# Output projection of a hybrid decoder layer: its last two column parts as one part of 1024 columns, with seven products for four pairs of k-tiles

## The chip, the cores and the metric

The kernel runs on one core of a Trainium2 chip. The time is device microseconds (us) from the start to the end of one execution. Before the change it is 1035.69 us, the median of 3 runs (1035.39 to 1035.95).

## The reference, cut to what matters

One decoder layer on a sequence of 256 tokens with model width 2048, everything in float32. Two attention blocks (A: dilated sliding windows, B: latent attention, each 8 heads of 128 columns) give `mixed`, 256 tokens by 2048 columns, of which block A is the first 1024. Then comes the part that the change touches, and the feed-forward part after it:

```python
mixed = jnp.concatenate([a_out.reshape(B, S, DSWA_HEADS * HEAD_DIM),
                         b_out.reshape(B, S, MLA_HEADS * V_HEAD_DIM)], axis=-1)
x = x + _rmsnorm(mixed @ w_out[layer], norm_attn_post[layer])      # w_out: 2048 x 2048

h = _rmsnorm(x, norm_mlp_pre[layer])
u = jnp.square(jax.nn.relu(h @ w_up[layer]))                       # w_up: 2048 x 8192
x = x + _rmsnorm(u @ w_down[layer], norm_mlp_post[layer])          # w_down: 8192 x 2048
```

## The kernel before, in words

**Precision by three products.** TensorE multiplies a rounded format here. Every float32 operand is therefore split into two tiles, `hi` (the rounded value, written by ScalarE) and `lo` (what is left, written by VectorE: `lo = raw - hi`), and every product is three matmuls: hi·hi, lo·hi, hi·lo (`split` L308, and `split_gain` L314 where a gain is multiplied in). A matmul takes 128 rows of k, 128 tokens and 512 columns. The two blocks of 128 tokens are called b = 0 and b = 1, a k-tile is 128 rows of a weight.

**The stream of weights.** `Weights` (L180 on) holds all weight tiles of the kernel as one planned list. A tile is 128 x 1024 numbers; its loading is one DMA of 512 KB on SP's queue into one of 5 `raw` buffers, and its split fills one of 8 `hi` and one of 8 `lo` buffers. `get(i)` (L227), called just ahead of the matmuls that use tile i, writes into the program all loads and splits up to tile i + 6 (`W_AHEAD`), never more than 8 tiles beyond the first one that is not yet done with. So the place of a split in VectorE's and ScalarE's program is six tiles ahead of its use; each engine works through its own program in the order written.

**The order of everything else.** A `Flow` counts the time of the matmuls written so far. Chains of other work (the softmax of a head, the evacuation of a result) are generators; a `yield 1.5` means that the next step is written into the program when the count has gone on by 1.5 us. `flow.pump()` behind each group of three matmuls writes what is due.

**The output projection** (L915 to L939). `mixT` (hi and lo) holds `mixed` transposed, 16 k-tiles. `w_out` is cut in four column parts n = 0 to 3 of 512 columns, each of 8 tiles of two k-tiles. The parts 0 and 1 run together, first the k-tiles 0 to 11, then 12 to 15, since the last heads of block B are still being computed meanwhile. Then part 2 runs, then part 3. In part 3 the last five tiles are done for b = 0 first, then for b = 1, so that the work on b = 0 can begin 30 matmuls before the end. Every part accumulates in one PSUM bank for each b.

At the first finished result the pool `pb` of block B is given back, and the gain `g_post` (1 MB, one row sent to 128 partitions) is loaded by SP's queue into the room that was freed (L930). `powers` (L848) starts there too: four squares of `g_post` on ScalarE, small operations, and four multiplications of 128 x 1024 of the residual `x` on VectorE (L869). `out_evac` (L831) takes a finished bank: a square with its sum on ScalarE (L835), a multiplication by `g_post` on VectorE (L836). When a b has all four parts, `residual(b)` (L872) computes the norm, updates `x`, and transposes it for the up projection, whose first five k-tiles run for b = 0 ahead of b = 1.

**Seven products.** The up and the down projection already use Strassen's scheme (in Winograd's form) for some pairs of k-tiles. A pair of k-tiles, two blocks of tokens and two halves of 512 columns are a 2 x 2 block product; instead of 8 block products it takes 7, of three matmuls each. For that, `seven` (L351) makes two tiles `t` and `u` of sums of the raw weights on VectorE and gives the stream four tiles: `b11` (half a tile), `b`, `u` and `t`. The operands on the left need four sums of blocks, split too. Three of the four results are had only from four extra accumulators m1, m6, m7, m5, which `close` (L1110) turns into three tiles that are added to the banks once. `seven_products` (L1094) writes the 21 matmuls.

Of the kernel before, what the change touches and what calls it, by code (L numbers as in the profile page):

```python
# [18 lines left out]
F32 = mybir.dt.float32  # L19
# [94 lines left out]
UP_STEPS = [up_steps(range(16))] + [THREE] * 7  # L114

# [153 lines left out]
def layer(nc, tc, io):  # L269
    flow = Flow()  # L270

    def pool(name, side, **kw):
        return tc.alloc_tile_pool(name=name, bufs=1, side=side, **kw)
# [70 lines left out]
    for n, m in ((0, 6), (1, 6), (0, 2), (1, 2), (2, 8), (3, 8)):  # L344
        ch_o[n].plan(m)
# [75 lines left out]
    wide_u, after = [], 0  # L421
# [307 lines left out]
    kv_chain = flow.start(latent(ckv, 0, "kv", lat), 2.0)  # L729
# [4 lines left out]
    pb = pool("pb", "right")  # L734

# [15 lines left out]
    latT["q"] = [pb.tile([P, 4, S], F32R, name=f"cqT_{w}") for w in ("hi", "lo")]  # L751
# [70 lines left out]


# [89 lines left out]

    res = [None] * NB
    for ns in ((0, 1), (2,), (3,)):  # L915
        if len(ns) == 2:
            order = [(c, t, b) for ts in (range(6), range(6, 8)) for c in range(2) for t in ts for b in range(NB)]
        else:
            order = [(0, t, b) for t, b in in_order(8, (0, APART[0] if ns == (3,) else 0))]
        for c, b, acc in proj(mixT, [ch_o[n] for n in ns], f"o{ns[0]}", order, heads_done):  # L920
            n = ns[c]
            if not late:
                flow.finish(*pair_chain)
                pb.release()
# [3 lines left out]
                po = late["po"] = pool("po", "right")  # L928
                late["g_post"] = po.tile([P, D], F32, name="g_post")
                nc.sync.dma_start(out=late["g_post"],  # L930
                                  in_=io["norm_attn_post"].partition_broadcast(P).rearrange("p o d -> p (o d)"))
                late["yg"] = [po.tile([P, D], F32, name=f"yg{b}") for b in range(NB)]
                pw_chain = flow.start(powers())
            out_evac(n, b, acc[0])
            if n == 3:
                flow.finish(pw_chain)
                weights.ahead = AHEAD_NORM
                res[b] = flow.start(residual(b), b * D_SECOND)
                flow.pump()  # L939
# [149 lines left out]
    def three(out, a, w, first, last):  # L1089

        for i, (x, y) in enumerate(((0, 0), (0, 1), (1, 0))):
            mm(out, a[x], w[y], first and i == 0, last and i == 2)

    def seven_products(ts, left, accs, m, first, last, m_first=False):  # L1094

        (a11, a12, a22), (s3, s1, s2, s4) = left
        prods = ((a11, 0, 0, 1), (a12, 1, 0, (0, 0)), (s4, 1, 1, (0, 1)), (s2, 2, 0, 6), (a22, 2, 1, (1, 0)),
                 (s3, 3, 1, 7), (s1, 3, 0, 5))
        if m_first:
            prods = sorted(prods, key=lambda x: not isinstance(x[3], int))  # L1100
        for p, (a, i, half, to) in enumerate(prods):
            w = weights.get(ts[i])
            in_m = isinstance(to, int)
            three(m[to] if in_m else accs[to], a, [w[x][:, half * 512:half * 512 + 512] for x in range(2)],
                  in_m and first, in_m and last)
            if all(x[1] != i for x in prods[p + 1:]):
                weights.free(ts[i])
            flow.pump()

    def close(c, m):  # L1110

# [279 lines left out]
```

## Time and profile before

| | before |
|---|---|
| median of the runs | 1035.69 us |
| profiled execution: its own time | 1035.85 us |
| profiled execution: span of the instructions | 1034.1 us |
| TensorE busy | 1022.4 us, 99% |
| VectorE busy | 834.4 us, 81% |
| ScalarE busy | 634.6 us, 61% |
| GpSimd busy | 63.5 us, 6% |
| first and last matmul of the output projection start at | 254.3 and 354.8 us |
| matmuls of the output projection | 384 |

The span runs from the first to the last instruction; 1.75 us of the execution's own time lie around it. "PE" is TensorE, "DVE" VectorE, "ACT" ScalarE, "POOL" GpSimd, "SP" the engine that issues most transfers. The trace shows a matmul as 389 ns long while the next starts 0.227 us later, because they overlap; the start-to-start time is what counts. Likewise a VectorE operation's record overlaps a little with the next one.

### The profile page before, as it was taken

What the parts mean: (1) busy time and instruction counts of PE and PEld (TensorE: products, weight loads), DVE (VectorE), ACT (ScalarE), POOL (GpSimd) and SP (SyncE); (2) the same over time, 40 slices, a digit from 0 to 9 for tenths busy, and PEclk for the clock granted to TensorE, in tenths of its full rate; (3) what the DMA queues carried; (4) which work ended last, traced back from release to release, by engine and by line L of the source; (5) the groups of instructions that cost most, each with busy time, mean ns of one, the idle gap of its engine ahead of it and who ended that gap; (6) DMA issues with size and microseconds to landing.
All of it is one profiled execution on the core that took longest, in us unless ns stands there. A gap on an engine that the chain in (4) does not pass through costs nothing.

```text
span 1034.1 us, 13262 instructions
## 1 busy us (share of the span) xinstructions
PE 1022.4 (99%) x4718; PEld 851.3 (82%) x4718; DVE 834.4 (81%) x1125; ACT 634.6 (61%) x850; POOL 63.5 (6%) x100
## 2 busy tenths in 40 slices
PE   9999999999999999999999999999999999999996
PEld 6888889889888878888888888888888888888885
DVE  6675536577547669999999999898999999899795
ACT  6585536566446467666775767666666665767571
POOL 0000000000001010000100100000101000211100
PEclk9999999999999999999999999999999999999998
DMA  8975447554438478877989887589989867888962
GB/s 288 361 237 166 138 136 223 155 163 144 144 122 263 142 276 284 272 239 258 285 258 302 269 262 258 191 275 335 354 267 366 299 240 258 302 314 303 329 240 82
DMA packets 105298, 253.44 MB, mean 245 GB/s; under 512 B 8720, under 2 KB 29712, under 8 KB 104848
## 3 DMA queue, kind: packets, MB, share of 16 engines
q1 hardware_dynamic: 65744, 175.14, 50.8%
q0 software_dynamic: 16112, 57.68, 16.8%
q10 hardware_dynamic: 23376, 19.78, 6.1%
q8 instruction: 37, 0.61, 0.2%
q14 instruction: 29, 0.24, 0.1%
HBM read 224.78 MB, written 27.79 MB: 244 GB/s over the span
## 4 chain that ended last, share of the span: by engine, by line
PE 96%; DVE 1%; DMA 1%; issue 1%; ACT 0%; POOL 0%; DVEq 0%; POOLq 0%; SPq 0%; ACTq 0%
PE acc_u L301 26%; PE y L301 25%; PE acc_o L301 8%; PE md L301 6%; PE m L301 6%; PE acc_v L301 4%; PE acc_qk L301 4%; PE acc_ckv L301 2%; PE acc_ukv L301 2%; PE acc_q L301 2%; PE acc_cq L301 2%; PE acc_k L301 2%; PE acc_uq L301 2%; PE sc_b L301 1%; DMA raw<-in_w_in 1%
## 5 line engine op out<-in xcount | busy, mean ns | idle before, releaser
L312 DVE TENSOR_TENSOR lo<-raw,hi 128x1024 fp32r<-128x1024 f32 (+3 forms) x207 | 234.1, 1149 | 83.9 <-ACT hi L311 82.5
L311 ACT ACTIVATE hi<-raw 128x1024 fp32r<-128x1024 f32 (+3 forms) x207 | 203.4, 996 | 70.9 <-DMA raw<-in_w_in 16.8
L301 PE MATMUL acc_u<-hi,hT_lo 128*128 128x512 f32 x386 | 150.3, 389 | 0.4 <-DVE hT_lo L312 0.4
L301 PE MATMUL acc_u<-hi,hT_hi 128*128 128x512 f32 x386 | 150.7, 390 | 0.0
L301 PE MATMUL acc_u<-lo,hT_hi 128*128 128x512 f32 x386 | 150.2, 389 | 0.0
L301 PE MATMUL y<-hi,uhi 128*128 128x512 f32 x358 | 139.3, 389 | 0.0
L301 PE MATMUL y<-lo,uhi 128*128 128x512 f32 x358 | 139.3, 389 | 0.0
L301 PE MATMUL y<-hi,ulo 128*128 128x512 f32 x358 | 139.3, 389 | 0.0
L315 ACT ACTIVATE hi<-raw,gcol 128x1024 fp32r<-128x1024 f32 x86 | 97.0, 1148 | 33.1 <-PE acc_u L301 18.2
L316 DVE SCALAR_TENSOR_TENSOR lo<-raw,gcol,hi 128x1024 fp32r<-128x1024 f32 x86 | 106.7, 1273 | 9.4 <-ACT hi L315 9.3
L301 PEld LDWEIGHTS acc_u<-hi,hT_lo 128*128 128x128 f32 x386 | 72.5, 188 | 15.9 <-DVE hT_lo L312 0.8
L301 PEld LDWEIGHTS acc_u<-lo,hT_hi 128*128 128x128 f32 x386 | 72.5, 188 | 14.9
L301 PEld LDWEIGHTS acc_u<-hi,hT_hi 128*128 128x128 f32 x386 | 72.5, 188 | 14.7
L301 PEld LDWEIGHTS y<-hi,uhi 128*128 128x128 f32 x358 | 67.2, 188 | 14.1
L301 PEld LDWEIGHTS y<-lo,uhi 128*128 128x128 f32 x358 | 67.2, 188 | 13.9
L301 PEld LDWEIGHTS y<-hi,ulo 128*128 128x128 f32 x358 | 67.2, 188 | 13.9
L312 DVE TENSOR_TENSOR lo<-st_down,hi 128x1024 fp32r<-128x1024 f32 x46 | 55.0, 1219 | 0.6 <-ACT hi L311 0.6
L301 PE MATMUL acc_o<-hi,mixT_hi 128*128 128x512 f32 x128 | 51.8, 405 | 0.0
L311 ACT ACTIVATE hi<-u 128x1024 fp32r<-128x1024 f32 (+1 forms) x33 | 32.2, 979 | 29.7 <-PE acc_u L301 11.7
L301 PE MATMUL acc_o<-hi,mixT_lo 128*128 128x512 f32 x128 | 50.2, 392 | 0.0
L301 PE MATMUL acc_o<-lo,mixT_hi 128*128 128x512 f32 x128 | 50.0, 390 | 0.0
L311 ACT ACTIVATE hi<-st_down 128x1024 fp32r<-128x1024 f32 x46 | 47.8, 1049 | 3.5 <-DVE st_down L371 2.1
(338 smaller groups left out, 2018.9 us busy)
## 6 DMA issues: line engine op xcount, KB each, us to landing
raw<-in_w_up SPq DMA_DIRECT2D x86, 512.0 KB, 4.8
raw<-in_w_down SPq DMA_DIRECT2D x82, 512.0 KB, 6.1
raw<-in_w_in SPq DMA_DIRECT2D x55, 512.0 KB, 5.1
ab<-in_w_up POOLq DMA_DIRECT2D x17, 1024.0 KB, 7.4
raw<-in_w_out SPq DMA_DIRECT2D x32, 512.0 KB, 4.4
ab_down<-in_w_down POOLq DMA_DIRECT2D x11, 1024.0 KB, 8.9
ulo<-ukeep POOLq DMA_DIRECT2D x20, 512.0 KB, 6.4
rkeep<-r ACTq DMA_DIRECT2D x28, 256.0 KB, 3.4
```

Source lines behind the costliest of these rows:

```text
L301: nc.tensor.matmul(out, a, b, start=start, stop=stop)
L311: nc.scalar.activation(hi, src, AF.Copy)
L312: nc.vector.tensor_tensor(out=lo, in0=src, in1=hi.bitcast(F32), op=OP.subtract)
L315: nc.scalar.activation(hi, src, AF.Copy, scale=g)
L316: nc.vector.scalar_tensor_tensor(out=lo, in0=src, scalar=g, in1=hi.bitcast(F32), op0=OP.mult, op1=OP.subtract)
```

## The change

The parts 0 and 1 stay as they are. The parts 2 and 3 become one part of 1024 columns. Its weights are loaded by k-tile (128 rows of 1024 columns, 512 KB each). Its order is: k-tile 8; then the pairs of k-tiles (0, 1), (2, 3), (4, 5), (6, 7), which are block A, by seven products each; then k-tiles 9 and 10; then the tail of k-tiles 11 to 15, for the four results (b, n) one after another. Each of those results is one PSUM bank of the banks 4 to 7; the extra accumulators m are in the banks 0 to 3.

New work beside the matmuls: `out_sums`, a chain started with parts 0 and 1, makes the sums of the left operands for the four pairs. The sums of the weights are made by `seven`, each pair from two loaded raw tiles, with the tiles `ckv` and `cq` as room for `t` and `u`. After the fourth pair `close` makes the three tiles, and four additions on VectorE bring them into the banks: the one for (0, 0) behind that bank's matmuls of k-tile 10, the others during the tail. In the fourth pair the products for m come first. `residual(0)` starts behind the result (0, 1), 30 matmuls before the end.

Some tiles change their place: the junk of `latent` shares a buffer with the rotary temporaries (`rp1`), the q latents `cqT` move from `pb` to a pool `lat2`, `lat` is given back later, and `hT` is allocated behind the last use of that room.

```diff
+OUT_STEPS = [("k", 8), ("w", 0), ("w", 1), ("w", 2), ("w", 3), *(("k", k) for k in range(9, 16))]
+OUT_TAIL = 5
...
-    for n, m in ((0, 6), (1, 6), (0, 2), (1, 2), (2, 8), (3, 8)):
+    for n, m in ((0, 6), (1, 6), (0, 2), (1, 2)):
         ch_o[n].plan(m)
...
+    def out_weight(k):
+        return io["w_out"][k * P:(k + 1) * P, CW:]
+
+    def seven_out(kp):
+        return seven(lambda: [weights.load(out_weight(2 * kp + i), CW, f"raw_o{kp}{i}") for i in range(2)],
+                     lambda: late["tu"])
+
+    wide_o, after = [], 0
+    for what, k in OUT_STEPS:
+        if what == "k":
+            ts = [weights.plan(out_weight(k), 1, CW)]
+        else:
+            ts, after = plan_seven(*seven_out(k), after)
+        wide_o.append((what, k, ts))
...
-            junk = pl.tile([P, 512], BF16, tag="junk", bufs=1, name=f"junk_{n}{b}")
+            junk = pl.tile([P, 512], BF16, tag="rp1", bufs=1, name=f"junk_{n}{b}")
...
-    latT["q"] = [pb.tile([P, 4, S], F32R, name=f"cqT_{w}") for w in ("hi", "lo")]
+    ost = lat2.tile([P, 2, CW], F32R, name="ost")
+    latT["q"] = [lat2.tile([P, 4, S], F32R, name=f"cqT_{w}") for w in ("hi", "lo")]
...
+    late["tu"] = [t.rearrange("p b n -> p (b n)")[:, :CW] for t in (ckv, cq)]
+    osts = [ost[:, 0], ost[:, 1], *(t.rearrange("p k s -> p (k s)") for t in latT["q"])]
+    osums = []
+    def out_sums():
+        tt = nc.vector.tensor_tensor
+        f = pb.tile([P, 512], F32, tag="kb", bufs=1, name="f_out")
+        q = pb.tile([P, NB, 384], F32, tag="qb", bufs=2, name="q_out").rearrange("p b n -> p (b n)")[:, :512]
+        fs, qs = [x.rearrange("p (k s) -> p k s", s=P) for x in (f, q)]
+        for kp in range(4):
+            st = [osts[kp][:, i * 512:(i + 1) * 512] for i in range(2)]
+            hs = [t[:, 2 * kp:2 * kp + 2, :].rearrange("p k s -> p (k s)") for t in mixT]
+            tt(out=f, in0=hs[0].bitcast(F32), in1=hs[1].bitcast(F32), op=OP.add)
+            tt(out=qs[:, 0], in0=fs[:, 0], in1=fs[:, 1], op=OP.subtract)
+            tt(out=qs[:, 3], in0=fs[:, 1], in1=fs[:, 3], op=OP.subtract)
+            yield 1.5
+            tt(out=qs[:, 1], in0=qs[:, 0], in1=fs[:, 3], op=OP.add)
+            tt(out=qs[:, 2], in0=fs[:, 2], in1=qs[:, 1], op=OP.subtract)
+            yield 1.5
+            nc.scalar.activation(st[0], q, AF.Copy)
+            yield 1.5
+            tt(out=st[1], in0=q, in1=st[0].bitcast(F32), op=OP.subtract)
...
+            yield 4.0
...
+    out_chain = flow.start(out_sums(), 1.0)
+    order = [(c, t, b) for ts in (range(6), range(6, 8)) for c in range(2) for t in ts for b in range(NB)]
+    first_bank = turn[0] + 1
+    for n, b, acc in proj(mixT, ch_o[:2], "o0", order, heads_done):
...
+        out_evac(n, b, acc[0])
+    flow.finish(out_chain)
+    accs = {(b, n): bank(4 + 2 * b + n, f"acc_o{2 + n}_{b}") for b, n in PARTS}
+    m = {i: bank((first_bank + o) % 4, f"m{i}_o") for o, i in enumerate((1, 6, 7, 5))}
...
+    for t, (what, k, tiles) in enumerate(wide_o[:-OUT_TAIL]):
+        if what == "k":
+            w = weights.get(tiles[0])
+            for b, n in PARTS:
+                out_mm(k, w, b, n, t == 0)
+                flow.pump()
+                if t == len(wide_o) - OUT_TAIL - 1 and (b, n) == (0, 0):
+                    nc.vector.tensor_tensor(out=accs[b, n], in0=accs[b, n], in1=more[b, n], op=OP.add)
+            weights.free(tiles[0])
         else:
+            blocks = [[tok(mixT[x], 2 * k + kk, bb) for x in range(2)] for kk, bb in ((0, 0), (1, 0), (1, 1))]
+            seven_products(tiles, (blocks, osums[k]), accs, m, k == 0, t == last_pair, t == last_pair)
+            if t == last_pair:
+                more = close(out_c, m)
+    for i, (b, n) in enumerate(PARTS):
+        for t, (what, k, tiles) in enumerate(tail):
+            w = weights.get(tiles[0])
+            three_more(accs[b, n], [tok(mixT[x], k, b) for x in range(2)], [w_[:, 0, n * 512:n * 512 + 512] for w_ in w])
...
+            for nb in PARTS[1:2] if (i, t) == (0, 0) else PARTS[2:] if (i, t) == (1, 0) else ():
+                nc.vector.tensor_tensor(out=accs[nb], in0=accs[nb], in1=more[nb], op=OP.add)
+            flow.pump()
+        out_evac(2 + n, b, accs[b, n])
+        if n:
...
+            weights.ahead = AHEAD_NORM
+            res[b] = flow.start(residual(b), b * D_SECOND)
+            flow.pump()
```

More of the change, by code (lines that the diff above doesn't have):

```diff
@@ L734, in layer @@
     pb = pool("pb", "right")
+    lat2 = pool("lat2", "left")
     krT = pb.tile([P, 2, S], F32, name="krT")
@@ L927, in layer @@
                 late["hT"] = [hp.tile([P, KD, S], F32R, name=f"hT_{w}") for w in ("hi", "lo")]
[L928 to L939, printed above, removed]
+            weights.ahead = AHEAD_NORM
+            res[b] = flow.start(residual(b), b * D_SECOND)
+            flow.pump()
     hT = late["hT"]
```

94 lines of the change are left out of this document (54 added, 40 removed).

## The prediction

> **What bounds the kernel now.** First the page: share of each engine, and who is on the chain that ended last.
>
> ```profile
> span 1034.1 us, 13262 instructions
> PE 1022.4 (99%) x4718; PEld 851.3 (82%) x4718; DVE 834.4 (81%) x1125; ACT 634.6 (61%) x850; POOL 63.5 (6%) x100
> ...
> PE 96%; DVE 1%; DMA 1%; issue 1%; ACT 0%; POOL 0%; DVEq 0%; POOLq 0%; SPq 0%; ACTq 0%
> ```
>
> TensorE is the bound, so a matmul less is a gain, and a wait of TensorE anywhere is a loss of its whole length, as nothing later has room to give it back. Then the waits of TensorE from 240 to 400 us, the one row of the chain of waits inside the projection, and the busy time by stretches (columns: TensorE, its weight loads, VectorE, ScalarE, GpSimd, clock, DMA):
>
> ```profile
> PE acc_u L301 <- DVE hT_lo L312: 0.4, 1, 0.4
> PE qrt L305 <- DVE qT L777: 0.2, 1, 0.2
> ```
> ```profile
> 302.52 49.95 PE acc_o L301 x219
> ```
> ```profile
> 264.00:304.00 40.00, 40.00 (x196) 33.22 (x194) 20.89 (x48) 19.03 (x37) 0.00 (x0) 1.00 0.31 96
> 304.00:338.50 34.50, 34.50 (x154) 28.55 (x153) 23.30 (x32) 19.85 (x34) 4.61 (x6) 1.00 0.84 270
> ```
>
> TensorE waits 0.6 us in 160, and goes through 219 matmuls in 49.95 us, 0.228 us each, at full clock. VectorE has a third to a half of its time free. So what counts is whether VectorE's added work fits not into its mean but into the order in which it is written.
>
> **The gain.** Four pairs, 21 matmuls for 24: 12 x 0.228 = 2.74 us less. Weights, bytes and transfers stay: 16 transfers of 512 KB for the parts 2 and 3 before, 8 + 4 x 2 after.
>
> **The cost: VectorE's queue up to the first addition.** I count the weight tiles from 0 at the start of the projection: 0 to 15 are parts 0 and 1, 16 is k-tile 8, 17 to 20, 21 to 24, 25 to 28, 29 to 32 are b11, b, u, t of the four pairs, 33 to 39 the k-tiles 9 to 15, 40 the first of the up projection. The addition into (0, 0) is written behind `get(34)`, which has written everything up to tile 40. VectorE works in order, so tile 40 is split ahead of that addition, and TensorE's tail cannot start without it.
>
> The rows for VectorE's start (`g_post` lands; then splits that wait for ScalarE, which waited for raw tiles):
>
> ```profile
> 307.62 1.29 DVE L836 TENSOR_TENSOR yg<-acc_o,g_post 128x512 f32<-128x512 f32 x2 [4.02 <-DMA g_post<-in_norm_attn_post]
> 310.60 2.60 DVE L312 TENSOR_TENSOR lo<-raw,hi 128x1024 fp32r<-128x1024 f32 x2 [1.69 <-ACT hi L311]
> ...
> 320.04 0.15 DVE L855 TENSOR_REDUCE gg<-gg 128x1 f32<-128x4 f32 x1
> ...
> 320.57 1.23 DVE L312 TENSOR_TENSOR lo<-raw,hi 128x1024 fp32r<-128x1024 f32 x1
> 322.38 0.17 DVE L859 TENSOR_SCALAR pw<-rstd_pw 128x2 int32<-128x2 int32 x1 [0.58 <-POOL rstd_pw L506]
> ...
> 323.21 0.75 DVE L869 TENSOR_SCALAR x<-x,pw 128x1024 f32<-128x1024 f32 x1
> 323.87 1.22 DVE L312 TENSOR_TENSOR lo<-raw,hi 128x1024 fp32r<-128x1024 f32 x1
> 325.01 0.75 DVE L869 TENSOR_SCALAR x<-x,pw 128x1024 f32<-128x1024 f32 x1
> ```
> ```profile
> 305.64 0.60 ACT L835 ACTIVATE junko<-acc_o 128x512 bf16<-128x512 f32 x1 [0.67 <-PE acc_o L301]
> 306.13 0.19 ACT L835 ACTIVATION_READ_ACCUMULATOR junko<-acc_o 128x1 f32 x1
> 309.51 1.06 ACT L311 ACTIVATE hi<-raw 128x1024 fp32r<-128x1024 f32 x1 [3.18 <-DMA raw<-in_w_out]
> 310.88 1.06 ACT L311 ACTIVATE hi<-raw 128x1024 fp32r<-128x1024 f32 x1 [0.31 <-DMA raw<-in_w_out]
> ```
>
> and for the pieces of one pair, of `close`, and of the first split of the up projection:
>
> ```profile
> 437.49 2.87 DVE L1116 TENSOR_TENSOR c<-m,c 128x512 f32<-128x512 f32 x4
> 440.28 2.47 DVE L316 SCALAR_TENSOR_TENSOR lo<-raw,gcol,hi 128x1024 fp32r<-128x1024 f32 x2
> 442.67 2.48 DVE L1178 TENSOR_TENSOR acc_u<-acc_u,c 128x512 f32<-128x512 f32 x4
> 445.06 0.68 DVE L312 TENSOR_TENSOR lo<-ab,hi 128x512 fp32r<-128x512 f32 x1
> 445.66 1.22 DVE L366 TENSOR_TENSOR t<-ab 128x1024 f32<-128x1024 f32 x1
> ...
> 453.41 1.22 DVE L366 TENSOR_TENSOR t<-ab 128x1024 f32<-128x1024 f32 x1
> 454.66 0.69 DVE L370 TENSOR_TENSOR u<-t,ab 128x512 f32<-128x512 f32 x1
> 455.38 0.69 DVE L371 TENSOR_TENSOR u<-u,ab 128x512 f32<-128x512 f32 x1
> 456.00 2.47 DVE L316 SCALAR_TENSOR_TENSOR lo<-raw,gcol,hi 128x1024 fp32r<-128x1024 f32 x2
> ```
>
> Start to start: split 323.87 to 325.01, 1.14 us; split with gain (442.67 - 440.28) / 2 = 1.20; half split (b11) 0.60; x by pw 0.66; reduction block 0.53; pw block 0.83; `close` 2.79; an addition (445.06 - 442.67) / 4 = 0.60. The sums of a pair took 453.41 to 456.00, 2.59; here t comes from two operations of 512 in place of one of 1024, so 2.65. A pair costs VectorE 2.65 + 0.60 + 3 x 1.14 = 6.67 us and TensorE 21 x 0.228 = 4.79, and four pairs stand in a row.
>
> How far ahead can VectorE be? `g_post` lands at 307.6, and behind its wait stand the two evacuations, then tile 20 and the sums of the second pair (tiles 21 to 24). Their raw tiles are SP's next transfers behind `g_post`, as they were before, so I let them land with the rows at 309.51 and 310.88. Evacuations to 308.8, tile 20 to 310.0, sums (second operation at 310.9) to 312.9, tile 21 to 313.5, the other two evacuations to 314.7. From there without a gap:
>
> - tiles 22 to 24: 3.42; third pair 6.67; fourth pair 6.67
> - `powers`, which by its yields falls between the second and fourth pair: 0.53 + 0.83 + 4 x 0.66 = 4.00
> - tiles 33 to 37: 5.70; `close` 2.79; tiles 38, 39: 2.28; tile 40: 1.20; addition 0.60
>
> Sum 33.3, so the first addition ends at 348.0. TensorE: b = 1 of part 0 ends at 305.6 (ScalarE's row that waited for it), 24 matmuls more end at 311.1; k-tile 8, four pairs, k-tiles 9 and 10 are 12 + 84 + 24 = 120 matmuls, 27.4 us, so it would begin the tail at 338.5. It waits 9.6 us, in two places. Tiles 31 and 32 come out of VectorE at 330.8 and 332.0, wanted at 328.9 and soon after: 2.4 us. Then 27 matmuls to 340.9 at 0.228, and 7.2 us for the addition. ScalarE is no bound: four tiles of at most 1.06 us are 4.2 us a pair.
>
> Bounds of this term. VectorE cannot pass the last evacuation earlier than 311.1 + 0.8 (ScalarE's two rows) + 0.6 = 312.5; behind it the same 33.3 us, to 345.8: at least 7.3 us. Above, raw tiles that land 1.5 us later: 11.1. I take 9.6.
>
> **The sums of the left operands.** `out_sums` writes three groups a pair on VectorE: one operation of 512 and two of 128; two of 128; one of 512. Most of it falls into the free half of 264 to 304. The first two groups of the first pair are due 1.0 and 2.5 us behind the start of the projection, a little later for the steps of three matmuls, and that is between these rows:
>
> ```profile
> 257.37 0.55 DVE L637 TENSOR_SCALAR s_b<-s_b,st_b 128x128 f32<-128x128 f32 x2
> 257.84 0.42 DVE L615 TENSOR_TENSOR rp_qr<-qb,trig 128x256 f32<-128x256 f32 x1
> 258.18 0.28 DVE L616 TENSOR_TENSOR rp_qr<-qb,trig 128x128 f32<-128x128 f32 x1
> 258.38 0.28 DVE L617 TENSOR_TENSOR rp_qr<-qb,trig 128x128 f32<-128x128 f32 x1
> 258.69 0.42 DVE L618 TENSOR_TENSOR qr<-rp_qr,rp_qr 128x256 f32<-128x256 f32 x1
> 259.04 1.22 DVE L312 TENSOR_TENSOR lo<-raw,hi 128x1024 fp32r<-128x1024 f32 x1
> 260.17 0.68 DVE L777 COPY qT<-qt 128x512 f32<-128x512 f32 x1
> ```
> ```profile
> 260.91 0.44 PE L305 MATMUL qrt<-ident,qr 128*128 128x128 f32 x2 [0.19 <-DVE qT L777]
> ```
>
> There VectorE has no gap, and TensorE already waits for its copy `qT`; the transposes `qrt` cannot go on before. An operation of 512 is 0.60 us as above, one of 128 is 0.20 by itself and 0.31 where the next waits for it (rows of 258.18 and 258.38); so 0.60 + 0.25 + 0.25 and 0.25 + 0.30 push that copy back by 1.65 us. Bounds 0 (the steps fall behind the copy) and 1.65; I take 1.5. The later pairs' steps I count at nothing: VectorE is idle for 19 of the 40 us from 264 on. Were that cover gone, each would cost what it takes, 2.3 us a pair.
>
> **The clock.** The only matmuls of the trace that follow a long rest are the first:
>
> ```profile
> 1.19 3.38 PE L526 MATMUL warm<-zero 128*128 128x512 bf16 x8 [1.19 <-DVE zero L523]
> ```
>
> 8 matmuls of 512 columns in 3.38 us, 0.42 each, against 0.228: 1.5 us lost. The waits quoted above are 0.4 us at most, so the trace doesn't show from which length on a rest does this. Bounds 0 and 1.5; a rest of 7 us is nearer to the start than to any other row, so 1.5.
>
> [...]
>
> **What costs nothing.** The junk in `rp1`: its readers and writers are far apart. The later release of `lat`: `hT` is first written behind the result (0, 1), the room's last use is the addition of `more` two results before. The last evacuations: (1, 0) puts 0.8 us on ScalarE and 0.6 on VectorE into `residual(0)`, which has 30 matmuls, 6.8 us, of cover as before; gone, it costs up to 0.6. The banks of m are evacuated by 314.7, wanted from 313.8 (m1, evacuated first) to 318 (m5). SP issues `g_post` one raw tile earlier in its list; it waits for `pb` either way.
>
> **Sum.** Profiled execution 1035.85 (span 1034.1 and 1.75 around it; 0.16 over the median): 1035.85 - 2.74 + 9.6 + 1.5 + 1.5 = 1045.7.
>
> **The rivals.**
>
> *The same queue, with less of the two small terms.* For it: no row shows the clock falling inside the span, and the chain steps may fall a little later. Without the clock 1044.2, without the early wait too 1042.7, with the lower bound of the queue 1035.85 - 2.74 + 7.3 = 1040.4.
>
> *More: raw tiles late.* The second pair's loads start behind `g_post`, in a stretch where DMA is at 0.84. With 11.1 for the queue 1047.2, and 0.6 for `residual(0)` 1047.8. Against it: five raw buffers are free then, as before.
>
> *Not slower: the splits stay ahead.* This is the addition's place in VectorE's program: if what stands ahead of it is done by 338.5, nothing is left but 12 matmuls, 1033.1. For it: the up projection has pairs too and TensorE doesn't wait there. It decides at 33.3 us of work against 338.5 - 314.7 = 23.8; 9.5 us would have to be gone or lie behind the addition. Against it: in the up projection k-tiles stand between the pairs, here none; a k-tile gives TensorE 2.7 us for 1.14 of VectorE, a pair 4.79 for 6.67.
>
> *No change.* The wait must be 2 to 5 us in all, below the lower bound.
>
> **How the numbers follow.** Forecast (1043.5 to 1047) 0.50; the smaller form of it (1040.4 to 1043.5) 0.30; late raw tiles 0.12; not slower 0.05; no change 0.03. About 0.2%, 2.1 us, is what a measurement here can tell from no change. Slower 0.92, same 0.03, faster 0.05. The range 1040.4 to 1048.0 leaves out the last two cases and a part of the late tiles.
>
> **What would show it.** Right: TensorE's waits in the projection name VectorE, about 2 us at the fourth pair's u and t (`hi`, `lo`) and about 7 at the first addition (acc_o from VectorE); VectorE is busy without a gap from about 314 for 33 us; the matmuls behind the long wait are slower for some us; `qrt` waits some 1.8 us for `qT`. Wrong: TensorE's row in the projection still runs through unbroken, or VectorE's stretch has gaps that wait for DMA, or the addition stands ahead of the splits of tiles 38 to 40.

## The result, and the profile after

The changed kernel takes 1049.07 us (median; 1046.33 to 1050.31), the kernel before 1035.82 beside it: a ratio of 1.0122, 95% interval 1.0099 to 1.0145. It is slower, by 13.2 us where 9.9 were forecast, and the median lies 1.1 us above the top of the range. The profiled execution took 1050.31. Its page, share of each engine and chain:

```profile
span 1048.5 us, 13307 instructions
PE 1025.9 (98%) x4706; PEld 851.4 (81%) x4706; DVE 863.8 (82%) x1181; ACT 641.7 (61%) x863; POOL 63.8 (6%) x100
...
PE 86%; DVE 6%; DMA 3%; issue 2%; ACT 2%; SPq 0%; ACTq 0%; POOL 0%; DVEq 0%; POOLq 0%
```

The 12 matmuls are gone (4718 to 4706), and TensorE's part of the chain has fallen from 96% to 86%. TensorE's waits from 240 to 400 us (what waits and what for; us in total, times, the longest):

```profile
PE acc_o L995 <- DVE acc_o L1033: 5.6, 1, 5.6
PE m_o L305 <- DVE lo L316: 1.9, 2, 1.7
PE qrt L309 <- DVE qT L798: 1.9, 1, 1.9
PE ht L309 <- DVE x L929: 0.5, 1, 0.5
PE acc_u L305 <- DVE hT_lo L316: 0.4, 1, 0.4
```

The first three rows are the three places that the prediction named: the first addition, the fourth pair's u and t, and `qrt` behind `qT`. VectorE's list between its last early evacuation and the first addition (start, duration, line, operation):

```profile
314.64 1.28 DVE L884 TENSOR_TENSOR yg<-acc_o,g_post 128x512 f32<-128x512 f32 x2
315.84 1.22 DVE L316 TENSOR_TENSOR lo<-raw_o,hi 128x1024 fp32r<-128x1024 f32 x1
...
319.36 0.69 DVE L373 TENSOR_TENSOR ckv<-raw_o 128x512 f32<-128x512 f32 x1
...
326.03 0.69 DVE L373 TENSOR_TENSOR ckv<-raw_o 128x512 f32<-128x512 f32 x1
...
345.05 2.35 DVE L316 TENSOR_TENSOR lo<-raw,hi 128x1024 fp32r<-128x1024 f32 x2
347.31 1.28 DVE L320 SCALAR_TENSOR_TENSOR lo<-raw,gcol,hi 128x1024 fp32r<-128x1024 f32 x1
348.51 0.69 DVE L1033 TENSOR_TENSOR acc_o<-acc_o,out_c 128x512 f32<-128x512 f32 x1
```
```profile
314.64:349.20 34.56, 27.18 (x109) 20.96 (x107) 34.04 (x49) 21.35 (x27) 4.93 (x6) 0.92 0.59 190
```

A pair takes 326.03 - 319.36 = 6.67 us of VectorE, as worked out. In the window row (TensorE, weight loads, VectorE, ScalarE, GpSimd, clock, DMA) VectorE is busy for 34.04 of 34.56 us; TensorE has 27.18. The addition is the last of the list, right behind the splits of tiles 38, 39 (345.05) and 40 (347.31); the next operation starts at 349.11. Now the stretches with the clock, and TensorE's own rows at the wait:

```profile
330.00:337.00 7.00, 5.10 (x15) 3.47 (x15) 6.90 (x13) 6.08 (x7) 2.27 (x2) 0.76 0.49 155
...
349.35:354.00 4.65, 4.65 (x11) 3.67 (x12) 2.83 (x3) 0.00 (x0) 0.00 (x0) 0.52 0.92 322
```
```profile
329.88 0.48 PE L305 MATMUL m_o<-hi,cqT_lo 128*128 128x512 f32 x1
332.10 0.50 PE L305 MATMUL m_o<-lo,cqT_lo 128*128 128x512 f32 x1 [1.74 <-DVE lo L316]
...
343.37 0.39 PE L305 MATMUL acc_o<-hi,mixT_lo 128*128 128x512 f32 x1
349.35 0.77 PE L995 MATMUL acc_o<-hi,mixT_hi 128*128 128x512 f32 x1 [5.59 <-DVE acc_o L1033]
349.91 0.63 PE L995 MATMUL acc_o<-lo,mixT_hi 128*128 128x512 f32 x1
...
353.75 0.44 PE L995 MATMUL acc_o<-lo,mixT_hi 128*128 128x512 f32 x1
```

At the addition the matmuls of 343.37 and 349.35 start 5.98 us apart where 0.23 is usual: 5.75 us lost. Behind it the clock is at 0.52, and matmuls start 0.427 us apart ((353.75 - 349.91) / 9); the ten intervals from 349.35 to 353.75 take 4.40 us in place of 2.28, 2.1 lost. At the fourth pair the wait loses 2.22 - 0.23 = 2.0, and there too the clock falls (0.76 over 330 to 337).

To compare kernels I cut each profiled execution at four points: the start of the first matmul into acc_o, of the first into acc_u, of the first into y, and of the last into y.

| Kernel | start of acc_o | projection | up projection | down projection |
|---|---|---|---|---|
| before | 254.3 | 101.0 | 337.5 | 332.3 |
| changed | 253.6 | 112.5 | 339.4 | 334.2 |
| changed, second profile (`e5_changed_again`) | 253.8 | 113.5 | 338.1 | 333.6 |

So 11.5 us of the 14.4 in the span are in the projection itself, and 3.7 behind it (0.7 are gained ahead of it). The part behind it goes down to 1.9 in the second profile, which is of the same code. One piece of it in the first profile, VectorE's row and TensorE's behind it near the end of the down projection:

```profile
983.29 1.23 DVE L370 TENSOR_TENSOR st_down<-ab_down 128x1024 f32<-128x1024 f32 x1 [5.92 <-DMA ab_down<-in_w_down]
```
```profile
987.16 0.50 PE L305 MATMUL y<-lo,uhi 128*128 128x512 f32 x1 [1.14 <-DVE lo L316]
```

A weight that landed late holds VectorE for 5.92 us and TensorE for 1.14.

### The profile page after: what moved, and what is told of

It is laid out like the page before. It is cut to its first block, busy times and chain, and to the rows that moved or that the text cites. A ratio compares the mean times of both kernels' runs of the same rounds, so it can differ in the third digit from the quotient of the medians.

```text
span 1048.5 us, 13307 instructions
## 1 busy us (share of the span) xinstructions
PE 1025.9 (98%) x4706; PEld 851.4 (81%) x4706; DVE 863.8 (82%) x1181; ACT 641.7 (61%) x863; POOL 63.8 (6%) x100
## 4 chain that ended last, share of the span: by engine, by line
PE 86%; DVE 6%; DMA 3%; issue 2%; ACT 2%; SPq 0%; ACTq 0%; POOL 0%; DVEq 0%; POOLq 0%
PE acc_u L305 24%; PE y L305 23%; PE md L305 5%; PE m L305 5%; PE acc_v L305 4%; PE acc_qk L305 4%; PE acc_o L305 3%; PE acc_ckv L305 2%; DVE lo L316 2%; PE acc_ukv L305 2%; PE acc_q L305 2%; PE acc_cq L305 2%; PE acc_k L305 2%; PE acc_uq L305 2%; DMA ab_down<-in_w_down 2%
## 5 line engine op out<-in xcount | busy, mean ns | idle before, releaser
L316 DVE TENSOR_TENSOR lo<-raw,hi 128x1024 fp32r<-128x1024 f32 (+3 forms) x199 | 224.0, 1146 | 76.8 <-ACT hi L315 76.2
L315 ACT ACTIVATE hi<-raw 128x1024 fp32r<-128x1024 f32 (+3 forms) x199 | 194.6, 994 | 66.5 <-DMA raw<-in_w_in 17.4
L305 PEld LDWEIGHTS acc_u<-lo,hT_hi 128*128 128x128 f32 x386 | 72.5, 188 | 16.2 <-DVE lo L320 1.4
L305 PE MATMUL md<-hi,s 128*128 128x512 f32 x138 | 50.0, 389 | 0.0
L316 DVE TENSOR_TENSOR lo<-u,hi 128x1024 fp32r<-128x1024 f32 (+1 forms) x33 | 36.5, 1118 | 5.7 <-ACT hi L315 5.6
L315 ACT ACTIVATE hi<-ab 128x512 fp32r<-128x512 f32 (+1 forms) x36 | 30.1, 840 | 17.6 <-PE acc_u L305 13.3
```

The source lines that it names most:

```text
L305: nc.tensor.matmul(out, a, b, start=start, stop=stop)
L315: nc.scalar.activation(hi, src, AF.Copy)
L316: nc.vector.tensor_tensor(out=lo, in0=src, in1=hi.bitcast(F32), op=OP.subtract)
```

## The experiments

The theory: in this stretch VectorE has more to do than TensorE, in a fixed order, and the first addition stands at its end. Rivals: the wide form itself costs (its buffers, its loads, its later releases); the order of the pairs; the clock; something that only a fourth pair in a row runs out of.

**`e1_wide_only`: the wide form without products.** All 16 k-tiles of the wide part are plain, so there are no sums, no `close` and no additions.

```diff
-OUT_STEPS = [("k", 8), ("w", 0), ("w", 1), ("w", 2), ("w", 3), *(("k", k) for k in range(9, 16))]
+OUT_STEPS = [("k", 8), *(("k", k) for k in range(8)), *(("k", k) for k in range(9, 16))]
...
-    out_chain = flow.start(out_sums(), 1.0)
```

> The one wide part with no pair by seven products: all 16 k-tiles (8, 0 to 7, 9 to 15) as plain tiles, no sums of left or right operands, no close, no additions; the tail, the moved tiles and the later evacuations stay. Queue theory (the loss comes from what the pairs put into VectorE's program ahead of the first addition, and the clock behind that wait): 384 matmuls as before, no wait of TensorE over 0.5 us in the projection, 1035 to 1037 us. Rival, the wide form (tail by four results, later evacuation, moved tiles) carries a good part of the 13 us: 1039 us or more. It also tells whether the waits of about 1 us each late in the up and down projection belong to the moved tiles: then they stay here.

Measured: 1036.9 us (1035.15 to 1039.75) beside 1036.55 of before, ratio 1.0005 (0.9995 to 1.0015). TensorE's waits from 240 to 420 us:

```profile
PE ht L309 <- DVE x L929: 0.5, 1, 0.5
...
PE qrt L309 <- DVE qT L798: 0.2, 1, 0.2
```

The projection takes 101.0 us, as before. The wide form is no cause of what the projection loses; that comes with the pairs. One row is new against the kernel before, and every wide kernel has it: 0.5 us of `ht` (the transposes of the normalized rows) behind `x`. The up projection is at least 0.5 us longer in each of them than before (338.1 here).

**`e2_sums_late`: the left sums out of the way of `qT`.**

```diff
-    out_chain = flow.start(out_sums(), 1.0)
+    out_chain = flow.start(out_sums(), 6.0)
```

> The sums of the left operands start 6.0 us behind the start of the projection in place of 1.0, so behind the copy qT; nothing else changes. Queue theory: the wait of the transposes qrt for qT falls from 1.9 us to 0.2, everything behind it is 1.7 us earlier, the wait at the first addition keeps its 5.6 us: 1.7 us less than the changed kernel, about 1047.3. Rival (that wait is made up for by the later wait at the addition, since VectorE sets the end there): no change, 1049.

Measured: 1045.77 us (1044.9 to 1046.88), ratio 1.0093 (1.0078 to 1.0108); the projection takes 110.4 us.

```profile
PE acc_o L995 <- DVE acc_o L1033: 7.2, 1, 7.2
PE m_o L305 <- DVE lo L316: 1.9, 2, 1.7
...
PE qrt L309 <- DVE qT L798: 0.2, 1, 0.2
```

The early wait is gone, so its cause is shown. The wait at the addition is longer here, since after the same wait of 1.7 us at the fourth pair the clock did not fall in this execution (1.00 from 330 to 337 us; row in the last section), and TensorE came earlier to an addition whose time VectorE sets. A slow stretch ahead of that wait costs nothing: from the projection's first matmul to the tail's first it is 94.0 us here, and in the changed kernel 95.7, which is 94.0 too without the 1.7 of `qrt`. The time fell by more than the 1.7 us expected (3.3 by the medians); the projection is 2.0 us shorter, and the rest of the difference lies in the stages behind it, which differ by nearly 2 us between the two profiles of the changed kernel as well.

**`e3_filler`: matmuls in place of the rest.** 24 matmuls whose result nobody reads stand ahead of the tail, 5.5 us at 0.228.

```diff
+    fill = bank(first_bank % 4, "fill")
+    for _ in range(24):
+        nc.tensor.matmul(fill, tok(mixT[0], 8, 0), mixT[0][:, 8:10, :].rearrange("p k s -> p (k s)"),
+                         start=True, stop=True)
```

> Adds 24 matmuls of 512 columns (5.5 us, their result is never read) between k-tile 10 and the tail, where TensorE waits 5.6 us for the first addition. Clock theory: the addition ends at the same time, TensorE's granted clock stays at 1.0 from 349 to 354, the first ten matmuls of the tail take 0.228 us each in place of 0.427: 2.0 us less, about 1047. Rival (the slow matmuls come from the addition's bank or VectorE's traffic, not from the rest): no gain, or a loss of up to 0.5 us.

Measured: 1046.14 us (1044.82 to 1047.84), ratio 1.0097 (1.0082 to 1.0112). The stretch behind the addition:

```profile
349.35:354.00 4.65, 4.23 (x19) 3.16 (x19) 4.46 (x5) 0.56 (x1) 0.00 (x0) 1.00 0.92 322
```

The clock is at 1.00 where it was at 0.52, and from the tail's first matmul to the first of the up projection it is 14.7 us, in place of 16.7 in the changed kernel and 16.2 in its second profile. So the slow matmuls behind the addition follow from the rest, and are a loss of their own, of 1.5 to 2.1 us. The median is 3.6 us under that of the changed kernel run again (`e5_changed_again`), but the intervals of the two ratios touch (up to 1.0112, from 1.011), and what goes beyond those 2 us is not explained by the added matmuls.

**`e4_ahead2`: the splits of later tiles behind the addition.** From the fourth pair on, only two tiles are written ahead, so that tiles 37 to 40 are split behind the addition.

```diff
+        if t == last_pair:
+            weights.ahead = 2
```

> From the fourth pair on splits are written two tiles ahead of their use in place of six, so the splits of tiles 37 to 40 (4.6 us of VectorE) stand behind close and the first addition in place of ahead of them; the work is the same. Program order theory: the wait at the first addition falls from 5.6 to about 1 us, the clock doesn't fall there, the later tiles come in time: 5 to 6.5 us less than the changed kernel, 1043 to 1044. Rival, total work theory (VectorE has more work in this stretch than time wherever it is written): the wait moves to the tail's tiles 37 to 39 or to the addition into (0, 1), and the time falls by less than 2 us.

Measured: 1042.91 us (1042.19 to 1043.26), ratio 1.0064 (1.0049 to 1.0079); the projection takes 106.8 us.

```profile
342.25 2.35 DVE L316 TENSOR_TENSOR lo<-raw,hi 128x1024 fp32r<-128x1024 f32 x2
344.52 0.69 DVE L1035 TENSOR_TENSOR acc_o<-acc_o,out_c 128x512 f32<-128x512 f32 x1
```
```profile
...
PE acc_o L995 <- DVE acc_o L1035: 1.1, 1, 1.1
```

The addition is 4.0 us earlier: 3 x 1.14 + 1.20 = 4.6 for the four splits, with a list that began 0.6 later. The wait falls from 5.6 to 1.1 us. So the place of these four splits is shown to be a cause of the wait; it isn't the whole loss, since 6.4 us are left, with the waits of `qrt` (1.85) and of the fourth pair (1.75 us, and the slow clock behind it, 0.77 from 330 to 337 us) as they were.

**`e5_changed_again`: the changed kernel beside the next ones.**

> The changed kernel as it is, so that the others of this call have it on the same chip, and to see what of its 13 us comes back. In its first profile 11.5 us were lost between the first matmul of the output projection and the first of the up projection, and 3 us more behind that, in waits of about 1 us each in the up and the down projection. Queue theory: the 11.5 us come back within 0.5. If the later waits are set by the change, they come back at the same two places; if they are chance (landing times of transfers), they are elsewhere or absent, and the median is 1046 to 1048.

Measured: 1049.78 us (1048.07 to 1050.48), ratio 1.0126 (1.011 to 1.0141), with waits of 6.0, 1.8 and 1.7 us at the same three places. In this execution the clock fell behind the 1.8 us of `qrt` as well (0.78 from 260 to 264 us).

**`e6_spread`: plain k-tiles between the pairs.** The order is k-tile 8, pair 0, k-tile 9, pairs 1 to 3, k-tile 10: the same work with one plain k-tile moved between the pairs.

```diff
-OUT_STEPS = [("k", 8), ("w", 0), ("w", 1), ("w", 2), ("w", 3), *(("k", k) for k in range(9, 16))]
+OUT_STEPS = [("k", 8), ("w", 0), ("k", 9), ("w", 1), ("w", 2), ("w", 3), *(("k", k) for k in range(10, 16))]
```

> Order of steps k8, pair 0, k9, pair 1, pair 2, pair 3, k10 in place of k8, four pairs, k9, k10; nothing else. Before the fourth pair TensorE then has 2.7 us more work for 1.1 us more of VectorE's. Queue theory: the wait of 1.9 us for the fourth pair's tiles falls to 0.5 or less and the slow clock behind it (1.6 us) goes, but the first addition ends when VectorE has done the same list, so the wait there grows by about as much: no change of the time within 1 us. Rival (each wait is a loss of its own): 3 to 3.5 us less.

Measured: 1048.6 us (1046.83 to 1051.37), ratio 1.0119 (1.0099 to 1.0139). The whole stays within about 1 us of the changed kernel, as a list of unchanged length says; the addition is at 348.81. (The first row below names ScalarE, but the addition ends at 349.50, 0.15 us ahead of the matmul that waited, as in the changed kernel.) But the wait at the fourth pair grew where it was to vanish:

```profile
PE acc_o L995 <- ACT hi L319: 5.9, 1, 5.9
PE m_o L305 <- DVE lo L316: 2.9, 2, 2.7
...
```
```profile
331.13 0.16 DVE L907 TENSOR_SCALAR pw<-rstd_pw 128x2 int32<-128x2 int32 x1
...
331.96 0.75 DVE L917 TENSOR_SCALAR x<-x,pw 128x1024 f32<-128x1024 f32 x1
332.62 1.22 DVE L316 TENSOR_TENSOR lo<-raw_o,hi 128x1024 fp32r<-128x1024 f32 x1
333.75 1.22 DVE L316 TENSOR_TENSOR lo<-cq,hi 128x1024 fp32r<-128x1024 f32 x1
```

The block of `powers` (0.83 us) and a multiplication (0.66) now stand ahead of the fourth pair's b, u and t; in the changed kernel they stand behind. My count of the queue for this variant had left out that the due times of other work move with the order. VectorE also came to this list later, after two waits of 0.4 us for ScalarE: the addition is 96.0 us behind the projection's first matmul here, and 94.9 in the changed kernel.

**`e7_two_pairs`: half of the pairs.** Pairs 0 and 1, and k-tiles 4 to 7 plain; the left sums of two pairs only.

```diff
+N_OUT = 2
-OUT_STEPS = [("k", 8), ("w", 0), ("w", 1), ("w", 2), ("w", 3), *(("k", k) for k in range(9, 16))]
+OUT_STEPS = [("k", 8), ("w", 0), ("w", 1), *(("k", k) for k in (4, 5, 6, 7)), *(("k", k) for k in range(9, 16))]
```

> Two pairs by seven products (k-tiles 0 to 3) and the k-tiles 4 to 7 as plain tiles; sums of the left operands for two pairs. Saves 6 matmuls, 1.4 us, against plain tiles. VectorE's list ahead of the first addition gets 13.3 us shorter by two pairs and 4.6 longer by four tiles, so 24.5 us: the addition ends at about 340, when TensorE is there too. Queue theory: no wait over 0.5 us at the addition and at the last pair, full clock; the early wait for qT (1.9 us) stays: 0 to 1.5 us over the kernel before. Rival (a cost of each pair that isn't in VectorE's list): half of the changed kernel's loss, 5 us or more over the kernel before.

Measured: 1038.19 us (1035.94 to 1038.92), ratio 1.0017 (1.0008 to 1.0027), 1.8 us by the ratio and 2.1 by the medians, a little above the 1.5 that were the most expected; the projection takes 103.1 us. There is no wait at the addition and none in a pair; `qrt` still waits 1.9 us, and behind it the clock falls, which the changed kernel's first profile had not shown there:

```profile
261.16 0.53 PE L310 MATMUL qrt<-ident,qr 128*128 128x128 f32 x2 [1.85 <-DVE qT L799]
```
```profile
260.00:264.00 4.00, 2.84 (x10) 2.37 (x10) 3.30 (x8) 1.58 (x2) 0.00 (x0) 0.67 0.40 131
```

**`e8_cand4`: four pairs with much of the list moved.** Late left sums, plain k-tiles between the pairs, one tile written ahead in the tail, the additions into (0, 0) and (0, 1) behind their tails, and the multiplications of x on ScalarE.

```diff
-OUT_STEPS = [("k", 8), ("w", 0), ("w", 1), ("w", 2), ("w", 3), *(("k", k) for k in range(9, 16))]
+OUT_STEPS = [("k", 8), ("w", 0), ("k", 9), ("w", 1), ("k", 10), ("w", 2), ("w", 3), *(("k", k) for k in range(11, 16))]
...
-                nc.vector.tensor_scalar_mul(xs[b][:, c], xs[b][:, c], pw[:, b:b + 1])
+                nc.scalar.activation(xs[b][:, c], xs[b][:, c], AF.Copy, scale=pw[:, b:b + 1])
...
-    out_chain = flow.start(out_sums(), 1.0)
+    out_chain = flow.start(out_sums(), 6.0)
...
+    weights.ahead = 1
...
+        if not b:
+            nc.vector.tensor_tensor(out=accs[b, n], in0=accs[b, n], in1=more[b, n], op=OP.add)
```

> All four pairs, with VectorE's list taken apart: order k8, pair 0, k9, pair 1, k10, pair 2, pair 3, tail; the additions into the two banks of b = 0 stand behind their tail, ahead of their evacuation, where TensorE doesn't wait for them; during the tail splits are written one tile ahead; the four multiplications of x are on ScalarE; the sums of the left operands start at 6.0 us. Program order theory: no wait over 0.7 us in the projection, full clock, and the 2.7 us of the 12 matmuls are kept but for up to 1 us of a later residual for b = 0: 1 to 2.5 us under the kernel before. Total work theory: VectorE is still late at the evacuations of b = 0, TensorE waits for hT: not under the kernel before.

Measured: 1041.25 us (1040.23 to 1041.73), ratio 1.0044 (1.0029 to 1.0059): 8.5 us better than the changed kernel, but not 1 to 2.5 us faster than the kernel before, as it would be if the order were all. The waits have moved, not gone:

```profile
PE acc_o L999 <- DVE acc_o L1052: 2.5, 1, 2.5
PE acc_u L306 <- DVE hT_lo L317: 1.3, 2, 0.9
PE m_o L306 <- DVE lo L317: 0.9, 2, 0.8
PE ht L310 <- DVE x L930: 0.8, 1, 0.8
...
```

All four wait for VectorE. This order doesn't mend it, and that none would is argued, not tried: a pair costs VectorE 6.67 - 2 x 1.14 = 4.4 us more than two plain tiles, four pairs with `close` and additions 17.6 + 2.8 + 2.4 = 22.8 us, for 2.74 us of matmuls.

**`e9_two_pairs_late`: two pairs and the late left sums.** The diffs of `e7_two_pairs` and `e2_sums_late` together.

```diff
+N_OUT = 2
+OUT_STEPS = [("k", 8), ("w", 0), ("w", 1), *(("k", k) for k in (4, 5, 6, 7)), *(("k", k) for k in range(9, 16))]
...
+    out_chain = flow.start(out_sums(), 6.0)
```

> Two pairs in place of four, k-tiles 4 to 7 plain, and the sums of the left operands begun 6 us later. In the run with two pairs the addition came 0.05 us before TensorE wanted it, and what was left was the wait of qrt for qT (1.9 us) and the slow matmuls behind it (1.5 us). Queue theory: with the sums out of the way of qT both are gone, VectorE's list begins earlier by as much as TensorE arrives earlier (in the run with late sums it moved by 1.8 us with TensorE), so the addition still fits; the projection takes 103.1 - 3.4 = 99.7 us, 1.3 under before, and with 0.6 us given back in the up projection the whole is 1035.0 to 1036.0, a ratio of 0.9985 to 1.0. Rival, a list that is fixed by the landing of g_post and not by TensorE: then what qrt gives free comes back as a wait of 1.5 to 3.4 us at the addition, and the time stays at 1037.5 to 1038.5, ratio 1.0015 to 1.0025.

Measured: 1035.57 us (1033.92 to 1036.99) beside 1035.97, ratio 0.9995 (0.9986 to 1.0004): no difference that can be told. The time is in the middle of what was expected, but not for the expected reason. `qrt` waits 0.2 us and the first addition is in time (TensorE goes on from k-tile 10 into the tail without a wait). But the projection takes 101.2 us, not 99.7, mostly for a wait of 1.1 us at the second addition:

```profile
338.54 0.69 DVE L1034 TENSOR_TENSOR acc_o<-acc_o,out_c 128x512 f32<-128x512 f32 x1
342.18 1.28 DVE L321 SCALAR_TENSOR_TENSOR lo<-raw,gcol,hi 128x1024 fp32r<-128x1024 f32 x1 [2.96 <-ACT hi L320]
343.39 0.69 DVE L1048 TENSOR_TENSOR acc_o<-acc_o,out_c 128x512 f32<-128x512 f32 x1
```

It stands behind the split of tile 41, whose `hi` ScalarE could begin only when the raw tile of `w_up` had landed (it had idled 4.64 us for it). VectorE stands still for 2.96 us with the addition queued behind. The prediction had looked only at the first addition; the second has the same fault with another cause, a transfer.

**`e10_three_pairs_late`: three pairs.** As `e9_two_pairs_late`, with three pairs and k-tiles 6 and 7 plain.

```diff
+N_OUT = 3
+OUT_STEPS = [("k", 8), ("w", 0), ("w", 1), ("w", 2), ("k", 6), ("k", 7), *(("k", k) for k in range(9, 16))]
```

> Three pairs in place of four, k-tiles 6 and 7 plain behind them, late sums as in the other run. Queue theory: a pair is 6.67 us of VectorE against 2 x 1.14 for two plain tiles, so each pair sets the addition back by 4.4 us, and takes 0.7 us from TensorE: 5.1 us of wait a pair, once two pairs just fit. Three pairs wait about 5 us at the addition, hardly at the third pair's u and t; 1036.1 - 2.05 + 5.1 + 0.6 = 1039.8, with slow matmuls behind the wait up to 1041.5, a ratio of 1.0035 to 1.005. Rival, that only the fourth pair in a row runs out of something (raw buffers, transfers): no wait over 1 us, 1034.5 to 1036, a ratio of 0.9985 to 1.0.

Measured: 1044.43 us (1041.0 to 1046.92), ratio 1.0101 (1.0085 to 1.0116). The profiled execution, 1041.0 us, has

```profile
PE acc_o L996 <- DVE acc_o L1034: 4.6, 1, 4.6
...
```

and no other wait of more than 0.5 us, none for u and t, so the step from two pairs to three is as long as the queue says (about 5 us forecast), and nothing runs out with the fourth pair only. The runs' median, however, is 3.4 us above that execution, outside of what I had forecast.

**`e11_three_filler` and `e12_three_again`: where those 3.4 us are.** The first has the 24 matmuls of `e3_filler` ahead of the tail of three pairs, the second is `e10_three_pairs_late` unchanged.

```diff
+    fill = bank(first_bank % 4, "fill")
+    for _ in range(24):
```

> Three pairs with late sums as before it, and 24 matmuls ahead of the tail whose result nobody reads (5.5 us at 0.228), so that TensorE works on while the addition is awaited. The run without them took 1041.0 us in its profiled execution and 1041.0 to 1046.9 (median 1044.4) over its runs. If the clock behind the wait makes that spread: the profiled tail runs at 0.228 a matmul, the wait at the addition is at most 0.6 us, and the runs lie between 1040 and 1042, their median 2 to 4 us under that of the same kernel without the matmuls. If transfers that land at different times make it: the spread and the median stay, 1041 to 1047, about 1044.

> The kernel with three pairs and late sums once more, beside the one with the added matmuls. The profile before it shows a wait of 4.6 us at the addition, ten slow matmuls behind it and 106.5 us for the projection in an execution of 1041.0. A second profiled execution nearer to the median of 1044.4 shows where the difference is: by the clock, a stretch of more than 2 us at half clock that the first one doesn't have, between 253 and 360; by the transfers, a longer wait at the addition or waits in the up projection.

Measured: with the matmuls 1041.16 us (1039.15 to 1043.06), ratio 1.0043 (1.0026 to 1.006); without 1041.91 (1040.73 to 1045.35), ratio 1.0059 (1.0039 to 1.0079). The second profile of three pairs repeats the first: 4.6 us of wait at the addition, 105.9 us for the projection. The median of 1044.4 did not come again, and the kernel before ranged from 1034.53 to 1039.76 beside these two. So neither answer is borne out: the two intervals overlap, and the spread with the added matmuls (3.9 us) is not clearly smaller than without (4.6). In the profiles the added matmuls do shorten the projection (105.0 us in place of 106.5 and 105.9), but in that one execution TensorE waits 1.6 us for a split in the up projection. Why that one set of runs lay higher stays open. Its three longest runs, 1045.7 to 1046.92 us, have the lowest granted clock (0.992 to 0.993 over the whole execution, 0.994 to 0.997 in the other three), so falls of the clock may be a part of it; they aren't all of it, as a run of 1041.11 us in the second set has 0.994 too.

## Why the prediction was right or wrong

**Right: direction, mechanism and places.** The first addition ends VectorE's gapless list, three splits of later tiles stand right ahead of it, and the waits name VectorE at the three places forecast. Undoing each alone takes away its wait, or most of it: the left sums (`e2_sums_late`), the splits ahead of the addition (`e4_ahead2`, 5.6 to 1.1 us), the pairs themselves (`e1_wide_only`, `e7_two_pairs`; with three pairs the wait for u and t is gone, `e10_three_pairs_late`).

**Right in size: the queue.** VectorE's list, from 315.84 to 349.11, took 33.3 us, as forecast; it began 1.1 us later than forecast, as TensorE was held up by `qrt` ahead of it. The projection lost 112.5 - 101.0 = 11.5 us net, so 14.2 with the 2.7 of the matmuls saved. Of these, 1.7 belong to `qrt` (forecast 1.5: the first two groups of `out_sums`, at 257.20 and 260.66, stand ahead of `qT` and take 1.13 and 0.53 us from start to start) and 2.1 to 2.2 to the matmuls behind the addition:

```profile
257.20 0.68 DVE L858 TENSOR_TENSOR f_out<-mixT_hi,mixT_lo 128x512 f32<-128x512 f32 x1
...
258.33 0.42 DVE L634 TENSOR_TENSOR rp_qr<-qb,trig 128x256 f32<-128x256 f32 x1
...
260.66 0.28 DVE L862 TENSOR_TENSOR q_out<-q_out,f_out 128x128 f32<-128x128 f32 x1
...
261.19 0.68 DVE L798 COPY qT<-qt 128x512 f32<-128x512 f32 x1
```

That leaves 10.3 us up to the addition, for which 9.6 were forecast. They are divided otherwise: 2.4 + 7.2 were to be waits; measured are 2.0 and 5.75 of wait, and most of the rest is the slow clock behind the first of them, which delays TensorE on its way to an addition that isn't ready anyway. Of `powers`, the reduction block (0.53 us) fell ahead of the fourth pair's last tiles and the rest behind them, all of it ahead of the addition, as counted.

**Too small: the clock.** Forecast 1.5 us (the upper bound, from the first matmuls of the trace); 2.1 to 2.2 measured behind the addition in this execution, 1.7 in the second profile. The bound was not one: the slow stretch of the trace's start is 3.4 us long with 8 matmuls, this one 4.5 us behind the wait (349.35 to 353.85, by the last section). And the sum had one such stretch; where the clock fell behind `qrt` too (`e3_filler`, `e5_changed_again`, `e7_two_pairs`), it is a second loss: up to the tail's first matmul `e5_changed_again` takes 1.6 us more than the first profile of the same code.

**The failed step: the sum ends with the projection, and holds the clock at one stretch of 1.5 us.** The second half is answered above: 1.7 to 2.2 us for that stretch, and in some executions one more of 1.6. The first half: the prediction put nothing on what comes behind the projection. `residual(0)` was looked at and has its cover; `residual(1)` and the stages beyond were not costed. The profiled execution lost 1.87 us in the up projection and 1.87 in the down projection, the second one 0.6 and 1.3. Of these, 0.5 to 0.6 us of the up projection come with the wide form in every profile of it (the wait of `ht` for x is 0.5), a fixed cost that the sum lacked; why x comes later there was not tried. The others differ between executions of one kernel, and one of them (1.14 us, above) is a weight that landed late; `e1_wide_only` had 1.2 us of it in the down projection as well and still timed like the kernel before, so they are not charged to the change. The kernel before has one profile, whose down projection is the shortest of all (332.3 us; 332.6 to 334.2 in the others), so a part of each of these differences may be that one execution. Added up for the profiled execution: 0.7 more for the queue, 0.7 for the clock, 0.2 for `qrt`, 3.7 behind the projection, less 0.7 ahead of it, make 4.6, and that is the distance from 1045.7 to 1050.3. For the second profile, 1049.7, the same sum is 0.7 for the queue, 1.8 for the clock, 0.2 for `qrt`, 1.9 behind the projection, less 0.6 elsewhere: 4.0.

**The range.** It ended at the sum with the upper bounds of the queue and of `residual(0)` (1047.8), with the clock held at 1.5. With 2.2 for the clock and 0.6 for the up projection those bounds reach 1049.1. That this is the median is luck: the queue took 10.3 us and not its bound of 11.1, and the rest of the time lies in the stages behind.

**The rivals.** "Not slower: the splits stay ahead" was to be decided by 9.5 us of work to be taken away from ahead of the addition. Two pairs in place of four take 8.8 us away and keep TensorE busy for 1.4 us more, and the addition then ended at 341.2 where TensorE's next matmul was due at 341.25 (`e7_two_pairs`): the point of decision holds. Late raw tiles were not what decided: VectorE has half a microsecond of gaps in its 34.56 us. The smaller form's claim that no row shows the clock falling inside the span held for the kernel before alone.

## What to carry to other kernels

Fewer matmuls are worth what the engine that prepares their operands has free in that very stretch and ahead of the operation that releases the next matmul: here 22.8 us of VectorE bought 2.74 us of TensorE, and only as many pairs are free as fit before the addition (two of four, which gained nothing that could be told). Write down the in-order list of the preparing engine up to each release, with what a prefetch depth puts ahead of it, and do so for every release, not the first alone. And behind each new wait put a further loss for the clock (1.5 to 2.2 us here where it fell, nothing where it stayed at 1.00), and a margin for the stages that have no slack.

## What the runs showed of the hardware that was not expected

**A wait of less than 2 us can drop TensorE's clock, and the same wait may not.** The changed kernel and `e2_sums_late` wait 1.74 and 1.73 us for the same tile of the fourth pair. The first is at 0.76 from 330 to 337 us (row in the section on the result); the second, from the same view:

```profile
330.00:337.00 7.00, 6.83 (x31) 5.30 (x30) 6.90 (x14) 3.59 (x5) 2.74 (x5) 1.00 0.52 161
```

The 1.85 us of `qrt` dropped it in `e3_filler`, `e5_changed_again` and `e7_two_pairs` (0.80, 0.78 and 0.67 over 260 to 264 us) and not in the first profile of the changed kernel, `e4_ahead2` and `e6_spread` (1.00 there); 2.5 us at an addition did not in `e8_cand4` (1.00 from 306.7 to 352 us). In the changed kernel the clock (the number behind the five engines) changes at 333.37, 336.78, 347.02 and 353.85 us:

```profile
329.95:333.36 3.41, 1.51 (x6) 0.70 (x6) 3.38 (x5) 3.41 (x4) 1.51 (x1) 1.00 0.73 222
333.37:336.77 3.40, 3.40 (x9) 2.63 (x10) 3.33 (x9) 2.68 (x4) 0.81 (x1) 0.50 0.22 86
336.78:347.01 10.23, 6.98 (x31) 5.42 (x29) 10.02 (x12) 4.45 (x5) 2.52 (x4) 1.00 0.79 258
347.02:353.84 6.82, 4.49 (x11) 3.56 (x12) 5.16 (x6) 1.15 (x1) 0.00 (x0) 0.50 0.89 299
```

The stretches between these changes are 1, 3 and 2 times 3.41 us long, and the one from the last of them to the next, at 1043.34 us, 202 times. The fourth pair's slow matmuls begin 1.3 us behind the end of its wait (332.10), and of the 6.83 us at half clock at the addition the first 2.3 lie in the wait.

How the waits lie against such steps is an estimate: the clock's changes in each execution, read from the window rows between 260 and 354 us to about 0.1 us, counted back in steps of 3.41 us. By it the wait of `qrt` lies inside one step in the three executions where it dropped the clock (falls at 262.4, 262.2 and 261.4 us, 0.2 to 0.5 us behind the wait), and the end of a step falls into it in the three where it did not (at 261.7 in the changed kernel, where the wait lasts from 260.07 to 261.93, at 262.1 in `e4_ahead2` and at 259.9 in `e6_spread`). But lying inside one step is not enough: by the same estimate the 1.73 us of `e2_sums_late` does as well, and the clock stayed at 1.00. No run here shows what decides it.

**TensorE's loss at a wait is longer than the wait shown.** The row of 349.35 shows 5.59 us where the starts are 5.75 further apart than usual, since the wait is counted from the end of the row before (0.39 us behind its start, where matmuls usually start 0.23 us apart).
